# Attention stage of a hybrid block: both turns of a group behind y_b, and whole y_b products in every second group of some units

## The chip, the cores and the metric

The kernel runs on one core of one Trainium2 chip, in float32 (products are done on operands split in a high and a low part). The metric is the device time of the whole program in microseconds (us): the median of three runs, and beside it one execution taken by the hardware profiler. The engines are TensorE (PE; its weight loads are listed apart as PEld), VectorE (DVE), ScalarE (ACT), GpSimd (POOL) and SyncE (SP, which issues most of the DMAs).

## The reference, cut to what matters

One layer, a sequence of 2048 positions, model width 1024. Three groups of eight heads attend with a window and a dilation each; a recurrent branch runs beside them; both are projected, gated and merged.

```python
DILATION_GROUPS = ((128, 1), (512, 4), (2048, 16))
...
proj = x @ w_in[l] + b_in[l]
q, k, v, g_attn, u_lru, g_lru, gate_logits = jnp.split(proj, SPLIT_POINTS, axis=-1)
...
for g, (window, dilation) in enumerate(DILATION_GROUPS):
    o_g, lse_g = dilated_band_attention(q[:, :, g], k[:, :, g], v[:, :, g], window, dilation)
...
wts = jax.nn.softmax(jnp.stack(lses, axis=0), axis=0)
attn = jnp.sum(wts[..., None] * jnp.stack(outs, axis=0), axis=0)
attn = attn.reshape(B, S, ATTN_OUT_WIDTH).astype(dt) * jax.nn.silu(g_attn)
y_a = attn @ w_attn_proj[l]
...
y_b = (h * jax.nn.silu(g_lru)) @ w_lru_proj[l]
...
merged = gates[:, :, 0] * y_a + gates[:, :, 1] * y_b
out = merged @ w_out[l] + b_out[l]
x = layer_norm(DEEPNORM_ALPHA * x + out, ln_gain[l], ln_bias[l])
```

In `dilated_band_attention` a block of 128 queries meets the keys of its own block and of the one before it within its residue class, under a band mask; p = exp(s - m), l = sum p, o = p v. The outputs are divided and combined by weights from m and l.

## The kernel before

The program goes through the projection (L639 and its neighbours), then the attention stage (about 1453 to 1778 us of the span), then a stage that finishes y_b, then y_a, the output product and the layer norm. The change lies in the attention stage.

That stage works on 48 **groups** G of four query blocks for a pair of heads. Four groups are a **unit** u = G // 4: one head pair and one dilation group. Units with u % 3 = 0 and 2 have predecessor blocks (keys of two blocks, a band of 192 columns); units with u % 3 = 1, dilation 16, have none (128 columns), and neither have the first blocks of the others (one block of dilation 1, four of dilation 4). A group has two score jobs j = 2G, 2G + 1 of two blocks each. A job goes through these steps:

- `scores` (PE, L992 without and L998 with a predecessor) writes two banks of PSUM, tags "s0" and "s1", two buffers each.
- `weigh` (once for each block): DVE adds the mask and takes the maximum (L1012), ACT takes the exponential and the sum (L1014). The result lies in one of six p buffers PT in SBUF, cut from one tile PB.
- `turn_p` (PE, L1029) transposes p into two PSUM banks, tags "t0" and "t1" with one buffer each, or "s0" and "s1" at the last job. `copy_p` copies them to SBUF: e = 0 on ACT (L1042), e = 1 on DVE (L1044), or on ACT for the odd job of a group with spreads.
- `values` (PE, L1061) multiplies by V into the bank tagged "o" (one buffer), for two jobs at once, and DVE copies it out (L1077).

Once a unit, `turn_ml` transposes its maxima and sums (mlt, L1082), in the same "o" bank. From these, weights are made later, and `spread` (PE, L1155, into "s0" and "s1" banks) spreads them over the rows; DVE multiplies (L240) and POOL adds the three dilation groups up. At most two spreads lie in a group: in G = 19 to 25, 31 to 37 and 43 to 48.

Beside that the stage has pieces of **y_b**: 32 products n of 512 positions by 128 columns, each in two **halves** of twelve matmuls (`yb_part`, L1231; four parts of three). The bank tagged "y" takes one product. When it is complete DVE multiplies it by the gate (`yb_done`, L1241). `yb_care` loads what comes next: the weights of the next product, split by POOL (`split_wl`), and, during the last product of 512 positions (n = 7 and 15), the next eight h tiles, split by POOL (`split_h`, L1206 and L1207), behind which one group rests from y_b.

The order of the work is the order of the code in a loop over G; nothing is scheduled behind it. On each engine the instructions run in this order and wait for buffers and results of others. Before, a group runs on PE: turn of 2G - 2, scores of 2G and of 2G + 1, turn of 2G - 1, values of 2G - 3 and 2G - 2, one half of y_b (from G = 4 on, except in rests) with the spreads between its parts, mlt.

## Time and profile before

| what | value |
|---|---|
| median of 3 runs | 2117.38 us (2115.23 to 2119.68) |
| the profiled execution's own time | 2116.21 us |
| its span | 2114.3 us |
| scores' maxima, DVE L1012, whole stage | 216 of 353 ns and 168 of 287 ns |
| exponentials, ACT L1014, whole stage | 384, 421 ns |
| products with h, PE L1231, whole stage | 505, 402 ns |
| turns, PE L1029, whole stage | 1200, 229 ns |

The rows of the profile are read like this: a row of a timeline has its start, its length, the engine, the line, the operation, the output and the inputs by the program's names, the shapes, a count, and in brackets the idle time ahead of it and what ended it. "128*64" is the part of TensorE's array that a weight load takes. "issue" means that the profile shows nothing that the engine waited for. Times of a window are busy time within it.

### The profile page before, as it was taken

The page shows a single profiled execution, that of the slowest core. Times are in us where ns is not written, and L with a number is a line of the kernel's source. Part 1 is how long each engine was busy: PE and PEld are TensorE (multiplying, and loading weights), DVE is VectorE, ACT ScalarE, POOL GpSimd, SP SyncE. Part 2 cuts the span into 40 slices and gives each one's busy share as a digit, 9 for nine tenths or more (in the row PEclk, how much of TensorE's full clock was granted, in tenths as well). Part 3 has the DMA queues.
Part 4 walks back from the last instruction along what each step waited for, and adds up shares of the span by engine and source line. Part 5 has one row for each costly group of instructions (what it writes and reads, how often), then busy time and mean ns, then how long its engine had stood idle before and what let it go on. Part 6 is the DMA issues. An engine that isn't in the chain of part 4 may idle for free.

```text
span 2114.3 us, 35689 instructions
## 1 busy us (share of the span) xinstructions
PE 2093.4 (99%) x12069; PEld 1714.0 (81%) x12069; DVE 1650.2 (78%) x2937; ACT 1205.9 (57%) x2502; POOL 765.7 (36%) x685
## 2 busy tenths in 40 slices
PE   9999999999999999999999999999999999999998
PEld 7888888888888888888888888887788888788886
DVE  8787987988989768677777878875667767887667
ACT  6456556467457556677677787775666664321100
POOL 2544653653754301111111111112547678521120
PEclk9999999999999999999999999999999999999999
DMA  7876976876877866566655666669789886774431
GB/s 223 255 225 189 273 221 202 257 231 216 250 242 225 288 194 183 191 205 175 206 190 175 207 204 206 188 208 271 201 219 251 236 236 187 239 242 152 154 100 70
DMA packets 259077, 443.36 MB, mean 210 GB/s; under 512 B 64352, under 2 KB 92032, under 8 KB 255824
## 3 DMA queue, kind: packets, MB, share of 16 engines
q1 hardware_dynamic: 242256, 408.64, 61.7%
q0 software_dynamic: 11744, 23.54, 5.9%
q10 hardware_dynamic: 4896, 8.92, 1.1%
q8 instruction: 96, 1.57, 0.3%
q14 instruction: 85, 0.70, 0.1%
HBM read 290.00 MB, written 150.99 MB: 209 GB/s over the span
## 4 chain that ended last, share of the span: by engine, by line
PE 59%; DMA 4%; POOL 1%; DVE 1%; issue 1%; ACT 0%; SPq 0%; ACTq 0%; POOLq 0%; DVEq 0%
PE q L639 33%; PE yb L1231 6%; PE o L1061 3%; PE z L1536 3%; PE z L1538 3%; PE z L1537 3%; PE pt L1029 2%; PE s L998 2%; PE ya L1504 1%; PE ya L1505 1%; PE ya L1503 1%; DMA wor<-in_w_out_dram 1%; PE g L500 1%; PE s L992 1%; DMA war<-in_w_f_dram 1%; DMA hx<-hb_scr 1%
## 5 line engine op out<-in xcount | busy, mean ns | idle before, releaser
L639 PE MATMUL q<-xT,hS 128*128 128x512 f32 x1632 | 504.8, 390 | 0.0
L639 PE MATMUL q<-xT,l 128*128 128x512 f32 x1088 | 423.5, 389 | 0.0
L639 PE MATMUL q<-xB,hA 128*128 128x512 f32 x1344 | 417.8, 392 | 0.0
L639 PE MATMUL q<-xB,l 128*128 128x512 f32 x944 | 367.9, 390 | 0.0
L639 PEld LDWEIGHTS q<-xT,hS 128*128 128x128 f32 x1632 | 304.8, 188 | 64.4 <-issue 1.8
L639 PEld LDWEIGHTS q<-xB,hA 128*128 128x128 f32 x1344 | 250.6, 188 | 56.4 <-issue 5.5
L639 PEld LDWEIGHTS q<-xT,l 128*128 128x128 f32 x1088 | 204.2, 188 | 42.5
L240 POOL TENSOR_TENSOR sw<-sw,sin 128x512 f32<-128x512 f32 x96 | 156.4, 1635 | 167.6 <-ACT sw L329 94.7
L639 PEld LDWEIGHTS q<-xB,l 128*128 128x128 f32 x944 | 177.4, 188 | 37.3
L240 POOL TENSOR_TENSOR y<-y,h 128x512 f32<-128x512 f32 x28 | 39.2, 1401 | 384.1 <-DVE h L541 354.4
L1014 ACT ACTIVATE pb<-pb 128x192 f32<-128x192 f32 (+1 forms) x384 | 160.6, 421 | 26.1 <-DVE pb L1012 26.1
L639 PE MATMUL q<-xB,hS 128*128 128x512 f32 x544 | 168.7, 391 | 0.8 <-DVE v L240 0.8
L639 PE MATMUL q<-xT,hA 128*128 128x512 f32 x544 | 167.9, 390 | 0.0
L284 ACT ACTIVATE hA<-wA 128x512 fp32r<-128x512 f32 x220 | 138.5, 635 | 28.4 <-DVE l L240 11.4
L1231 PE MATMUL yb<-hx,wl 128*128 128x512 f32 x576 | 149.7, 400 | 1.0 <-POOL hx L1207 0.8
L284 ACT ACTIVATE hS<-S 128x512 fp32r<-128x512 f32 x170 | 108.3, 637 | 67.1 <-DVE S L240 47.5
L240 POOL TENSOR_TENSOR l<-wA,hA 128x512 fp32r<-128x512 f32 x68 | 110.2, 1621 | 84.5 <-ACT hA L284 49.5
L1231 PEld LDWEIGHTS yb<-hx,wl 128*128 128x128 f32 x576 | 104.5, 188 | 30.4 <-issue 5.6
L639 PEld LDWEIGHTS q<-xT,hA 128*128 128x128 f32 x544 | 101.8, 188 | 21.8 <-issue 0.8
L639 PEld LDWEIGHTS q<-xB,hS 128*128 128x128 f32 x544 | 101.2, 188 | 22.1 <-issue 1.6
L328 ACT ACTIVATE sw<-y 64x512 f32<-64x512 f32 x96 | 60.6, 631 | 83.5 <-DVE y L583 79.3
L1507 POOL TENSOR_TENSOR me<-gA,me 128x512 f32<-128x512 f32 x30 | 47.3, 1592 | 158.6 <-DVE gA L1506 135.9
(213 smaller groups left out, 4370.5 us busy)
## 6 DMA issues: line engine op xcount, KB each, us to landing
wA<-in_w_in_dram SPq DMA_DIRECT2D x220, 256.0 KB
wl_scr<-l SPq DMA_DIRECT2D x102, 512.0 KB
l<-wl_scr SPq DMA_DIRECT2D x102, 512.0 KB
wS<-in_w_in_dram SPq DMA_DIRECT2D x102, 256.0 KB
wS<-in_w_in_dram POOLq DMA_DIRECT2D x68, 256.0 KB, 7.0
wlr<-in_w_f_dram SPq DMA_DIRECT2D x64, 256.0 KB
mg_scr<-y SPq DMA_DIRECT2D x59, 256.0 KB
v_scr<-vs SPq DMA_DIRECT2D x48, 256.0 KB
```

The source lines that it names most:

```text
L240: eng.tensor_tensor(out=out, in0=in0, in1=in1, op=op)
L284: act.activation(heads(h), heads(r, False), AF.Copy)
L328: act.activation(flat(sw)[lo_], flat(rw)[up_], AF.Copy, scale=scale)
L639: pe.matmul(bank, w[:, ks], x[:, kk, xx], start=(first and i == 0), stop=(last and i == 11))
L998: pe.matmul(bank[h][es, b, 0:BW], q[hs, n * P + 64 * e:n * P + 64 * e + 64], k_[hs, at + 64 * e:at + 64 * e + BW], start=True, stop=True)
L1014: act.activation(pp, pp, AF.Exp, scale=-1.0, bias=mm, accum_out=ll)
L1061: pe.matmul(o[hs, 2 * i + b, :], V[:, kb, 64 * h:64 * h + 64], ptb[:, b, 2 * h + x, :], start=(x == lo // P), stop=(x == 1))
L1231: pe.matmul(YB["t"], w[:, a, k], hx(8 * c + k)[:, b], start=(hf == 0 and m == 0), stop=(hf == 1 and m == 11))
L1507: (dve if i in (6, 7) else pool).tensor_tensor(out=ME[c][:, f], in0=ga, in1=ME[c][:, f], op=ALU.add)
L1536: pe.matmul(z, mh[:, k], w[:, 0, hs], start=(k == 0), stop=False)
L1537: pe.matmul(z, mh[:, k], w[:, 1, hs], start=False, stop=False)
L1538: pe.matmul(z, ml[:, k], w[:, 0, hs], start=False, stop=(k == 7))
```

## The change

The loop's order on PE becomes: scores of 2G and of 2G + 1, values of 2G - 4 and 2G - 3, y_b with the spreads between its parts, mlt, then both turns, that of 2G - 2 in the "s" banks and that of 2G - 1 in the "t" banks. A job's values so come one to two groups later than before. There are eight p buffers in place of six; one of them lies in a new tile PX, which also takes the maxima and sums. Two buffers take the copied turns in place of three. In units with predecessors the odd groups have both halves of y_b and the even ones none; units without predecessors keep a half in each group. In all 44 halves lie in the stage in place of 42. The rests stay. All lines of the attention stage's functions stand three lower in the kernel after (L1012 becomes L1015).

```diff
@@ -915,7 +915,7 @@
     w_p = stC.enter_context(tc.tile_pool(name="w_p", bufs=1, reuse_waits="tile"))
     OT = [big(f"Z{i}", [P, 2, S], F32, f"o{i}") for i in range(3)]
     PB = big("Z3", [P, 4096], F32, "pb")
-    PT = [PB[:, 576 * i:576 * i + 576] for i in range(6)]
+    PT = [PB[:, 576 * i:576 * i + 576] for i in range(7)]
     BW = 192
 
     def pdata(p, h, a, b):
@@ -943,11 +943,14 @@
         x, y = ((2, 0), (2, 1), (1, 1))[i] if hp % 2 == 0 else ((0, 0), (0, 1), (1, 0))[i]
         return OT[x][:, y]
 
+    PX = at_p.tile([P, 576 + 256], F32, name="px", bufs=1)
+    PT.append(PX[:, 0:576])
+
     def zeros():
-        z = PB[:, 0:3456].rearrange("p (i c) -> p i c", c=576)
+        z = PB[:, 0:4032].rearrange("p (i c) -> p i c", c=576)
         for a in (0, 256, 512):
             dve.memset(z[:, :, a:a + 64], 0.0)
-        pool.memset(PB[:, 3456:3712], 0.0)
+        pool.memset(PX, 0.0)
 
     zeros()
 
@@ -1003,8 +1006,8 @@
         u, n = divmod(m, 16)
         bank, lo = st.pop(("s", m))
         if n == 0:
-            ML[u] = PB[:, 3456 + P * (u % 2):3456 + P * (u % 2) + P]
-        p = PT[m % 6]
+            ML[u] = PX[:, 576 + P * (u % 2):576 + P * (u % 2) + P]
+        p = PT[m % 8]
         cs, mk = (slice(lo, 256), mask) if lo else (slice(0, BW), band)
         for h in range(2):
             mm, ll = (ML[u][:, 32 * k + 16 * h + n:32 * k + 16 * h + n + 1] for k in range(2))
@@ -1017,7 +1020,7 @@
     def turn_p(j, tag="t"):
 
         pt = [aps.tile([P, 2, 4, 64], F32, tag=f"{tag}{e}", name=f"pt{e}{j}", bufs=1 if tag == "t" else 2) for e in range(2)]
-        ptb = at_p.tile([P, 2, 4, P], F32, tag="pt", name=f"ptb{j}", bufs=3)
+        ptb = at_p.tile([P, 2, 4, P], F32, tag="pt", name=f"ptb{j}", bufs=2)
         los = []
         for b in range(2):
             p, lo = st.pop(("p", 2 * j + b))
@@ -1333,59 +1336,61 @@
             spreads.setdefault(e + 7 + (i + (hp < 2)) // 2, []).append((hp, c, g))
 
     rests = set()
+    def turn(j, tag):
+        turn_p(j, tag)
+        copy_p(j, 0)
+        copy_p(j, 1)
+
     for G in range(NG + 1):
         run(late)
+        if G < GY or G in rests or G == NG:
+            m = 0
+        elif G // 4 % 3 == 1:
+            m = 1
+        else:
+            m = 2 * (G % 2)
+        now_ = [halves.pop(0) for _ in range(m)]
+        parts = [(*divmod(t, 2), i) for t in now_ for i in range(4)]
+
+        def some(k):
+            for _ in range(k):
+                if parts:
+                    n, hf, i = parts.pop(0)
+                    yb_part(n, hf, i)
+                    if i == 3 and hf:
+                        yb_done(n)
+
+        two = spreads.get(G, [])
         if G < NG:
-            if G:
-                turn_p(2 * G - 2)
-                copy_p(2 * G - 2, 0)
-                copy_p(2 * G - 2, 1)
             scores(2 * G)
             weigh(4 * G)
             weigh(4 * G + 1)
             scores(2 * G + 1)
-            if G:
-                turn_p(2 * G - 1)
-                copy_p(2 * G - 1, 0)
-                copy_p(2 * G - 1, 1)
             weigh(4 * G + 2)
             weigh(4 * G + 3)
-            if G:
-                values([j for j in (2 * G - 3, 2 * G - 2) if j >= 0])
-        else:
-            turn_p(2 * G - 2)
-            copy_p(2 * G - 2, 0)
-            copy_p(2 * G - 2, 1)
-            turn_p(2 * G - 1, "s")
-            copy_p(2 * G - 1, 0)
-            copy_p(2 * G - 1, 1)
-            values([2 * G - 3, 2 * G - 2])
-            values([2 * G - 1], "s0")
+        if G > 1:
+            values([2 * G - 4, 2 * G - 3])
         for fn in todo.pop(G, ()):
             fn()
-        y = G >= GY and G not in rests and (G < NG or len(halves) % 2)
-        if y:
-            n, hf = divmod(halves[0], 2)
-            yb_part(n, hf, 0)
-            yb_part(n, hf, 1)
-        two = spreads.pop(G, [])
+        some(1)
         if len(two) == 2:
             spread(*two[0], "s0")
-        if y:
-            yb_part(n, hf, 2)
+        some(2)
         if two:
             spread(*two[-1], "s1")
-        if y:
-            yb_part(n, hf, 3)
-            if hf:
-                yb_done(n)
+        some(9)
         if G % 4 == 0 and G:
             turn_ml(G // 4 - 1)
-        if y:
-            yb_care(halves.pop(0))
-            if hf and n in (7, 15):
+        if G:
+            turn(2 * G - 2, "s")
+            turn(2 * G - 1, "t")
+        spreads.pop(G, None)
+        for t in now_:
+            yb_care(t)
+            if t in (15, 31):
                 rests.add(G + 1)
         now["n"] += 1
+    values([2 * G - 2, 2 * G - 1])
     assert not todo and not spreads, (todo, spreads)
     now["n"] += 1
     run(late)
@@ -1447,7 +1452,7 @@
         rest.setdefault(16 + i, []).append(lambda: prep_wo(*wo.pop(0)))
     more = {(13, 15, 17, 19)[i]: [(3, c, g) for g in (0, 2, 1)] for i, c in enumerate(CO)}
     r0 = halves[0]
-    assert r0 == 42, r0
+    assert r0 == 44, r0
     for t in halves:
         n, hf = divmod(t, 2)
         run(late)
```

On ACT at G = 10 and 11 (ptb is the copy of a turn, with its job's number; pb and px are the p buffers) before:

```order
L1042 ACTIVATE ptb17_14884<-pt017_14882 128x4x64
L1014 ACTIVATE pb_13962<-pb_13962 128x192 x4
L1042 ACTIVATE ptb18_14936<-pt018_14934 128x8x64
L1014 ACTIVATE pb_13962<-pb_13962 128x192 x4
L1042 ACTIVATE ptb19_14985<-pt019_14983 128x8x64
L1014 ACTIVATE pb_13962<-pb_13962 128x192 x4
L1042 ACTIVATE ptb20_15056<-pt020_15054 128x8x64
L1014 ACTIVATE pb_13962<-pb_13962 128x192 x4
```

and now:

```order
L1045 ACTIVATE ptb16_14892<-pt016_14890 128x4x64
L1045 ACTIVATE ptb17_14905<-pt017_14903 128x4x64
L1017 ACTIVATE pb_13962,px_13975<-pb_13962,px_13975 128x192 x8
L1045 ACTIVATE ptb18_14982<-pt018_14980 128x8x64
L1045 ACTIVATE ptb19_15003<-pt019_15001 128x8x64
L1017 ACTIVATE pb_13962,px_13975<-pb_13962,px_13975 128x192 x6
L1017 ACTIVATE px_13975<-px_13975 128x192 x2
```

Before, a copy and four exponentials take turns; now the copies of both jobs stand behind the eight exponentials of the group.

On DVE at the end of a group with two spreads, G = 22 (ISA rows with a band are the maxima; w are the spread weights, gB the product with the gate) before:

```order
L1012 ISA pb_13962<-s045_16298,band_171 128x192
L1012 ISA pb_13962 128x1
L1012 ISA pb_13962<-s145_16299,band_171 128x192
L1012 ISA pb_13962 128x1
L1077 COPY o1_13960<-o41_16337 128x2x128 x2
L240 TENSOR_TENSOR o1_13960<-o1_13960,w011_16364 128x512
L240 TENSOR_TENSOR o2_13961<-o2_13961,w020_16370 128x512
L1241 SCALAR_TENSOR_TENSOR gB8_16056<-gB8_16056,yb10_16229 128x512
L1044 COPY ptb44_16387<-pt144_16386 128x8x64
```

and now:

```order
L1015 ISA pb_13962,px_13975<-s045_16284,band_171 128x192
L1015 ISA px_13975 128x1
L1015 ISA pb_13962,px_13975<-s145_16285,band_171 128x192
L1015 ISA px_13975 128x1
L1080 COPY o1_13960<-o40_16302 128x2x128 x2
L240 TENSOR_TENSOR o1_13960<-o1_13960,w011_16319 128x512
L240 TENSOR_TENSOR o2_13961<-o2_13961,w020_16322 128x512
L1047 COPY ptb42_16329<-pt142_16328 128x8x64
```

The products by w and the copy of a turn's e = 1 part follow the maxima as before. The copy belongs to the group's own last piece now (job 42 is turned at the end of G = 22; before, job 44's copy opens G = 23), and the gate's product, which closes a y_b product, has moved to the odd groups.

On PE at G = 12, the first of a unit, from the piece ahead of the values to the next turn (o are the values, yb the y_b product) before:

```order
L1029 MATMUL pt023_15214<-ident_161,pb_13962 128x64
L1029 MATMUL pt123_15215<-ident_161,pb_13962 128x64
L1029 MATMUL pt023_15214<-ident_161,pb_13962 128x64
L1029 MATMUL pt123_15215<-ident_161,pb_13962 128x64
L1061 MATMUL o21_15243<-ptb21_15105,V_13884 64x128 x8
L1061 MATMUL o21_15243<-ptb22_15169,V_13884 64x128 x8
L1231 MATMUL yb04_15264<-hx0_13964,wl_13963 128x512 x12
L1082 MATMUL mlt2_15277<-ident_161,pb_13962 128x128
```

and now:

```order
L1001 MATMUL s025_15172<-qk1_13921 64x192 x2
L1001 MATMUL s125_15173<-qk1_13921 64x192 x2
L1001 MATMUL s025_15172<-qk1_13921 64x192 x2
L1001 MATMUL s125_15173<-qk1_13921 64x192 x2
L1064 MATMUL o20_15190<-ptb20_15105,V_13884 64x128 x8
L1064 MATMUL o20_15190<-ptb21_15126,V_13884 64x128 x8
L1085 MATMUL mlt2_15211<-ident_161,px_13975 128x128
L1032 MATMUL pt022_15215<-ident_161,pb_13962 128x64
L1032 MATMUL pt122_15216<-ident_161,pb_13962 128x64
```

The values follow the scores and not a turn, and no y_b product stands between the values and mlt, which shares their bank.

## The prediction

> **What bounds the kernel now.** I read the page first: the span, the busy shares and the chain of work that ended last.
>
> ```profile
> span 2114.3 us, 35689 instructions
> PE 2093.4 (99%) x12069; PEld 1714.0 (81%) x12069; DVE 1650.2 (78%) x2937; ACT 1205.9 (57%) x2502; POOL 765.7 (36%) x685
> PEclk9999999999999999999999999999999999999999
> PE q L639 33%; PE yb L1231 6%; PE o L1061 3%; PE z L1536 3%; PE z L1538 3%; PE z L1537 3%; PE pt L1029 2%; PE s L998 2%; PE ya L1504 1%; PE ya L1505 1%; PE ya L1503 1%; DMA wor<-in_w_out_dram 1%; PE g L500 1%; PE s L992 1%; DMA war<-in_w_f_dram 1%; DMA hx<-hb_scr 1%
> ```
>
> TensorE is busy 99% of the span at full granted clock, and the chain runs almost wholly through its lines. So the time moves by what TensorE gets less or more to do, or by what it newly waits for. The change lies in the attention stage. The second view is the busy time by stretches of it:
>
> ```profile
> 1454.00:1500.00 46.00, 41.32 (x597) 33.00 (x591) 32.23 (x160) 34.04 (x147) 31.59 (x46) 1.00 0.90 263
> 1500.00:1550.00 50.00, 50.00 (x683) 40.04 (x680) 32.98 (x143) 32.34 (x130) 16.10 (x19) 1.00 0.76 193
> 1550.00:1600.00 50.00, 49.45 (x613) 40.37 (x617) 37.29 (x163) 35.29 (x151) 33.91 (x44) 1.00 0.88 246
> 1700.00:1750.00 50.00, 48.96 (x620) 40.19 (x613) 35.33 (x161) 34.50 (x148) 38.59 (x50) 1.00 0.81 232
> ```
>
> The columns are length, then PE, PEld, DVE, ACT and POOL busy. Behind the start TensorE has hardly an idle microsecond here (50.00 of 50), while DVE and ACT are busy for two thirds. There is slack on them on average; what counts is whether it lies where the new order needs it. The third view is the timeline of TensorE's weight loads in one group of a unit with predecessor blocks (G=10). A row's start against the next row's start is what a piece costs with the passage behind it.
>
> ```profile
> 1540.15 0.58 PEld L1029 LDWEIGHTS pt<-ident,pb 64*128 64x128 f32 x16 [0.35 <-issue]
> 1540.80 1.18 PEld L998 LDWEIGHTS s<-qk 64*64 64x64 f32 x32
> 1542.26 0.58 PEld L1029 LDWEIGHTS pt<-ident,pb 64*128 64x128 f32 x16 [0.28 <-issue]
> 1542.91 1.73 PEld L1061 LDWEIGHTS o<-ptb,V 128*64 128x64 f32 x32
> 1544.81 2.62 PEld L1231 LDWEIGHTS yb<-hx,wl 128*128 128x128 f32 x12 [0.17 <-issue]
> 1547.77 0.58 PEld L1029 LDWEIGHTS pt<-ident,pb 64*128 64x128 f32 x16 [0.35 <-issue]
> ```
>
> The group takes 1547.77 - 1540.15 = 7.62 us: turn 0.65, scores 1.46, turn 0.65, values 1.90, half a product 2.96. Between the first load of the scores (1540.80) and the next turn that needs their weights there are 6.97 us.
>
> **The change part by part.**
>
> *The turns side by side.* Before, each turn stands between two pieces of another kind. The one place of before with two turns in a row is the last group:
>
> ```profile
> 1773.05 1.07 PEld L1029 LDWEIGHTS pt<-ident,pb 64*128 64x128 f32 x32 [0.35 <-issue]
> 1774.19 2.60 PEld L1061 LDWEIGHTS o<-ptb,V 128*64 128x64 f32 x48
> ```
>
> Two take 1774.19 - 1773.05 = 1.14 us against 2 x 0.65: 0.15 less. The new passage from scores to values is not in the trace; scores to turn costs 0.28 of idle and values to y_b 0.17, so I set it equal to scores to turn (bounds: 0.1 either way per group). 28 groups in which full bands are turned: **-4.2** (bounds -1.5 to -7). In units without predecessors (half the transposes, and passages between scores and turn that are short already, 0.24 from turn to scores at 1579.97 below) nothing.
>
> *The whole product in one.* Two halves run together save one passage in and one out: 24 loads follow each other at (2.62 - 0.19)/11 = 0.22 us. One product alone has values to y_b, 0.17 idle, and y_b to turn, 0.35 idle; a pair of groups has these once less, and values to turn instead, say 0.2: about 0.32 a pair. Six pairs have an even group without spreads: **-1.9** (bounds 0 and -3.1).
>
> The Trainium skill, TensorEngine Tiling (Array Packing), Tiling Modes, states that changing the tiling mode drains TensorE. By that rule each passage between row shapes (64\*64, 64\*128, 128\*64, 128\*128 in the rows above) costs a drain and the change, which has fewer of them, gains; the rows agree in sign, 0.35 and 0.28 idle at changes of shape and none inside a piece. By the rule alone the kernel would be faster, which is the first rival below; the sum does not rest on it.
>
> *A stall that goes.* Late in the stage a second turn waits for ACT, which is held up by work on the denominators:
>
> ```profile
> 1721.31 0.58 PEld L1029 LDWEIGHTS pt<-ident,pb 64*128 64x128 f32 x16 [1.17 <-ACT ptb L1042]
> 1705.60 0.58 PEld L1029 LDWEIGHTS pt<-ident,pb 64*128 64x128 f32 x16 [0.41 <-ACT ptb L1042]
> ```
>
> In the new order both turns follow their own banks' last readers by a product's length: **-1.6** for the two (0 to -1.6).
>
> *What the groups without y_b now wait for.* This is the term that decides. ACT and DVE in the same group G=10:
>
> ```profile
> 1541.83 0.36 DVE L1012 CUSTOM_DVE_ANT_0 pb<-s,band 128x192 f32<-128x192 f32 x1
> 1544.54 0.35 DVE L1012 CUSTOM_DVE_ANT_0 pb<-s,band 128x192 f32<-128x192 f32 x1
> 1544.93 0.69 DVE L1077 COPY o<-o 128x512 f32<-128x512 f32 x1
> ...
> 1542.23 0.46 ACT L1014 ACTIVATE pb<-pb 128x192 f32<-128x192 f32 x1 [0.67 <-DVE pb L1012]
> 1544.00 0.58 ACT L1042 ACTIVATE ptb<-pt 128x512 f32<-128x512 f32 x1
> 1545.80 0.45 ACT L1014 ACTIVATE pb<-pb 128x192 f32<-128x192 f32 x1
> ```
>
> DVE's first maximum starts 1.03 us after the scores' first load (1540.80), eight take 8 x 0.28 = 2.25. ACT's first exponential starts 1.43 after it; eight take 8 x 0.44 = 3.5. In the new program ACT has all eight ahead of the copies out of the turned banks, and the first turn lies in the banks that the next group's second scores need. So those scores can't start before 1.43 + 3.5 + 0.58 (copy) + 0.15 (the signal, an estimate; mlt below starts 0.05 after the copy that it waits for has ended) = 5.65 us after this group's scores. A group with y_b is over 8 us long, so nothing waits. One without it has, to that point, scores 1.46 + values 1.90 + turns 1.14 + the first half of the next scores 0.59 = 5.09: it waits 0.56. Where the values are those of blocks without predecessors (1.02) it is 1.3. Groups 14, 26, 38: 0.6 each, 10: 1.3. Group 12 has the transpose of the maxima and denominators (mlt) ahead of the turns, in the bank of the values, so it waits for DVE's copy of them, 1.1 us in two pieces there: 1.2. Sum **+4.3**.
>
> Groups 8, 32 and 44 have the same mlt behind a unit without predecessors. How this looks the trace shows at G=20, the group that has no y_b already:
>
> ```profile
> 1579.97 0.32 PEld L1029 LDWEIGHTS pt<-ident,pb 64*128 64x128 f32 x8 [0.35 <-issue]
> 1580.21 0.98 PEld L992 LDWEIGHTS s<-qk 64*128 64x128 f32 x16
> 1581.11 0.38 PEld L1029 LDWEIGHTS pt<-ident,pb 64*128 64x128 f32 x8
> 1581.56 0.85 PEld L1061 LDWEIGHTS o<-ptb,V 128*64 128x64 f32 x16
> 1582.58 0.30 PEld L1155 LDWEIGHTS w<-wh,sel 128*128 128x128 f32 x2 [0.17 <-DVE pb L1012]
> 1583.87 0.14 PEld L1082 LDWEIGHTS mlt<-ident,pb 128*128 128x128 f32 x1 [0.99 <-DVE o L1077]
> 1582.78 1.04 DVE L1077 COPY o<-o 128x512 f32<-128x512 f32 x1
> ```
>
> mlt stands 3.66 us behind the scores, because DVE's copy of the values (1.04) comes behind eight maxima; TensorE idles 0.99 for it. With 0.90 of scores and 1.02 of values and nothing else ahead, the wait is 1.45 at 8; at 32 and 44 two spreads follow and their multiplications on DVE (0.69 each) hold the banks of the next scores: 1.8 each. Sum **+5.1**.
>
> Groups 22, 24, 34 and 46 have two spreads. The next scores need the spreads' banks back, that is DVE: 1.03 + 2.25 + copy 1.1 + 2 x 0.69 = 5.8 us. TensorE is there after 1.46 + 1.02 to 1.90 + 0.77 (spreads) + 1.14 = 4.4 to 5.3: waits of 1.45, 0.8, 1.45 and 1.45, **+5.2**. All twelve: **+14.5**. The bounds: nothing, if the copies come ahead of need, and about double, if each wait also delays the next group's exponentials beyond what its y_b hides.
>
> *Groups of units without predecessors.* These keep one half each, but their two turns now come last, and DVE has the closing product with the gate (0.69) and a copy (0.42) ahead of the next second scores where a product ends; eight such groups x 0.36 = **+2.8** (0 to 4).
>
> *The first product after the rest.* POOL splits the eight h tiles of the next 512 positions back to back:
>
> ```profile
> 1580.96 0.61 POOL L1206 CAST hx<-hx 128x512 fp32r<-128x512 f32 x1 [6.30 <-PE s L992]
> 1595.09 1.30 POOL L1207 TENSOR_TENSOR hx<-hx 128x512 fp32r<-128x512 f32 x1
> ...
> 1587.40 1.24 PEld L1231 LDWEIGHTS yb<-hx,wl 128*128 128x128 f32 x6 [0.17 <-POOL hx L1206]
> 1595.05 1.23 PEld L1231 LDWEIGHTS yb<-hx,wl 128*128 128x128 f32 x6 [0.17 <-POOL hx L1206]
> ...
> 1708.14 2.59 PEld L1231 LDWEIGHTS yb<-hx,wl 128*128 128x128 f32 x12 [0.17 <-POOL hx L1206]
> ```
>
> They end at 1596.4. Before, the product's second half starts at 1595.05 and needs the last tile at its end. As a whole product it starts at 1587 again and its last quarter would need it about 1592 + spreads: some 2.7 us of wait here (2.5 to 3.5); the same at the next such place, behind 1708.14, where POOL's joins stand between: 2 (0 to 5). **+4.7**.
>
> *Ends.* The last values follow the loop alone with their copy, 1.2 with mlt. At the start POOL sets 832 columns to zero in place of 256 ahead of the first maximum, which waits for it today:
>
> ```profile
> 1455.50 0.33 POOL L950 MEMSET pb<- 128x256 f32 x1
> 1455.87 0.29 DVE L1012 CUSTOM_DVE_ANT_0 pb<-s,mask 128x128 f32<-128x128 f32 x1 [0.72 <-POOL pb L950]
> ```
>
> From 0.33 for 256 columns some 0.5 to 0.7 more, and no turn fills the first groups: 1. Together **+2.2**. That two halves of y_b move from the next stage into this one is even: their work is the same, and the next stage's stalls are set by its own loads (0, ±1).
>
> **Sum**: gains 4.2 + 1.9 + 1.6 = 7.7; losses 14.5 + 2.8 + 4.7 + 2.2 = 24.2; net +16.5. The profiled execution took 2116.2 us (span 2114.3 and 1.9 around it); that gives 2132.7. It lies 1.2 under the median of the runs shown, 2117.4, so that a median would be 2133 to 2134. I predict 2133.
>
> **The rivals.** *Only the passages count* (faster). The waits rest on the sequence of ACT's and DVE's work against an interval of 5.1 us that I put together from pieces; were it 0.6 us longer, or did the turned banks come free earlier, the commonest wait would be gone, and at 1.5 us longer all. For: ACT is busy only 32 of 50 us. Against: the 0.99 us at G=20 is such a wait, seen. Then -7.7 plus 2 for the ends: about 2109 to 2112.
>
> *Half the waits* (about even). If the exponentials overlap better in the short group and POOL's tiles come in time, 7 + 2.5 + 2 remain against 7.7: +4, about 2120.
>
> *The waits grow* (slower still). If the delayed second scores also delay that group's exponentials, and the tiles of POOL come 5 us late at both places, 24 to 30 more: 2140 to 2146.
>
> *The change doesn't do what it says.* The two turns lie next to each other in the program and the products are whole in the odd groups; that leaves this out but for the start.
>
> **How the numbers follow.** A measurement of this kernel tells about 0.2%, 4.2 us, from no change. Forecast, waits about as summed (+9 to +24): 0.52. Half the waits (-3 to +9): 0.20. Only the passages (-10 to -3): 0.14. Growing waits (over +24): 0.14. Range 2111 to 2142, which leaves out most of the last and of the passages' case. Faster: 0.13; within 0.2%: 0.13, most of the half case; slower: 0.74.
>
> **What would show it.** Right: weight loads of the second scores (L998, L992) in odd groups idle 0.5 to 1.5 us for ACT's copy of the turned tile or DVE's product by w; mlt rows with 1 us or more behind DVE's copy of o; the product behind each rest waiting 2 to 3 us for POOL; pairs of turns at 1.14; PE's busy time in 50 us windows some 2 us under 50. Wrong: windows at 50.00 with scores that name no releaser, or a stall that names a DMA. My sum would be wrong first in the interval of a short group, since the same 0.5 us counts in twelve of them.

## The result, and the profile after

The kernel after takes 2134.24 us in the median of four runs (2132.99 to 2136.62), the kernel before 2117.49 beside it (2115.23 to 2119.68): a ratio of 1.0081, 95% interval 1.0068 to 1.0094. The change makes the kernel 17 us slower. Run again beside later experiments it gave 1.0085 (1.0071 to 1.0098). The span of the profiled execution went from 2114.3 to 2131.5, by 17.2.

From the page of after, the span, the busy shares and the chain of work that ended last:

```profile
span 2131.5 us, 35687 instructions
PE 2098.2 (98%) x12069; PEld 1715.4 (80%) x12069; DVE 1636.5 (77%) x2927; ACT 1204.3 (56%) x2500; POOL 770.6 (36%) x689
PE yb L1234 5%; PE z L1541 3%; PE z L1543 3%; PE z L1542 3%; PE o L1064 2%; PE pt L1032 1%; PE ya L1509 1%; PE ya L1510 1%; PE ya L1508 1%; POOL hx L1210 1%; PE s L1001 1%; PE s L995 1%; DMA ga<-ga_scr 0%; POOL hx L1209 0%; ACT pb L1017 0%
```

TensorE has as many matmuls and 5 us more of busy time, and its share falls by a point. The chain of before ran through TensorE and a few DMAs; POOL's split of h (L1209, L1210) and ACT's exponentials (L1017) are new in it. The windows (length, then PE, PEld, DVE, ACT and POOL busy, then the granted clock, the DMA share and GB/s) show where:

```profile
1500.00:1550.00 50.00, 46.26 (x666) 37.31 (x664) 32.94 (x150) 32.32 (x133) 11.69 (x14) 1.00 0.76 198
1550.00:1600.00 50.00, 47.93 (x521) 38.60 (x521) 29.70 (x134) 28.87 (x128) 35.53 (x47) 1.00 0.81 224
1700.00:1750.00 50.00, 47.73 (x640) 38.58 (x639) 29.51 (x125) 30.07 (x117) 41.43 (x53) 1.00 0.84 224
```

Where TensorE was busy for 50.00, 49.45 and 48.96 us of 50, it now is for 46.26, 47.93 and 47.73. The clock is granted in full in these windows (1.00), so these are waits.

The end of G=13, a group with a whole product, and G=14, one without, weight loads of TensorE in the timeline of after (G=14 begins at 1543.34, G=15 at 1547.63):

```profile
1536.66 5.31 PEld L1234 LDWEIGHTS yb<-hx,wl 128*128 128x128 f32 x24 [0.17 <-issue]
1542.33 0.95 PEld L1032 LDWEIGHTS pt<-ident,pb 64*128 64x128 f32 x28 [0.35 <-PE yb L1234]
1543.34 1.18 PEld L1001 LDWEIGHTS s<-qk 64*64 64x64 f32 x32
1544.80 1.51 PEld L1064 LDWEIGHTS o<-ptb,V 128*64 128x64 f32 x28 [0.28 <-issue]
1546.48 0.83 PEld L1032 LDWEIGHTS pt<-ident,pb 64*128 64x128 f32 x24 [0.17 <-issue]
1547.23 0.33 PEld L1032 LDWEIGHTS pt<-ident,px 64*128 64x128 f32 x8
1547.63 0.53 PEld L1001 LDWEIGHTS s<-qk 64*64 64x64 f32 x16
1548.81 0.53 PEld L1001 LDWEIGHTS s<-qk 64*64 64x64 f32 x16 [0.65 <-ACT ptb L1045]
```

The new order is seen: a whole product as 24 loads without a gap, then two turns in one, then scores. Behind the group without y_b the second scores idle 0.65 us for ACT's copy. ACT in the same stretch, its first and last exponential and the copies:

```profile
1544.66 0.45 ACT L1017 ACTIVATE pb<-pb,px 128x192 f32<-128x192 f32 x1 [0.55 <-DVE px L1015]
...
1547.75 0.44 ACT L1017 ACTIVATE pb<-pb,px 128x192 f32<-128x192 f32 x1
...
1548.19 1.05 ACT L1045 ACTIVATE ptb<-pt 128x512 f32<-128x512 f32 x2
```

Eight exponentials run without a gap from 1544.66 to 1548.19, the two copies follow at once, and the second scores start behind the first of them: 5.47 us behind the group's first load (1548.81 - 1543.34), against 5.65 in the prediction. The other kinds of wait in short groups, the product behind the rest, the last group, and a wait far behind the stage:

```profile
1502.56 0.14 PEld L1085 LDWEIGHTS mlt<-ident,px 128*128 128x128 f32 x1 [1.47 <-DVE o L1080]
...
1517.73 0.53 PEld L1001 LDWEIGHTS s<-qk 64*64 64x64 f32 x16 [1.30 <-ACT ptb L1045]
...
1531.90 0.14 PEld L1085 LDWEIGHTS mlt<-ident,px 128*128 128x128 f32 x1 [1.47 <-issue]
...
1596.63 0.30 PEld L1234 LDWEIGHTS yb<-hx,wl 128*128 128x128 f32 x2 [1.17 <-POOL hx L1210]
1597.18 0.19 PEld L1234 LDWEIGHTS yb<-hx,wl 128*128 128x128 f32 x1 [0.26 <-POOL hx L1209]
1598.53 0.30 PEld L1234 LDWEIGHTS yb<-hx,wl 128*128 128x128 f32 x2 [1.16 <-POOL hx L1210]
...
1604.69 0.20 PEld L1001 LDWEIGHTS s<-qk 64*64 64x64 f32 x4 [0.44 <-DVE o L240]
1605.28 1.17 PEld L1001 LDWEIGHTS s<-qk 64*64 64x64 f32 x28 [0.40 <-DVE o L240]
...
1791.89 1.75 PEld L1064 LDWEIGHTS o<-ptb,V 128*64 128x64 f32 x32 [0.57 <-ACT ptb L1045]
1795.10 0.14 PEld L1085 LDWEIGHTS mlt<-ident,px 128*128 128x128 f32 x1 [0.98 <-PE w L1158]
1797.01 1.76 PEld L1064 LDWEIGHTS o<-ptb,V 128*64 128x64 f32 x32 [0.57 <-ACT ptb L1045]
...
1885.81 0.19 PEld L1541 LDWEIGHTS z<-wo,ms 128*128 128x128 f32 x1 [1.04 <-ACT ms L1527]
```

At 1502.56 (G=8) mlt waits for DVE's copy of the values; the 1.47 at 1531.90 (G=12) is the same place, and there the profile names nothing. At 1604.69 (G=22) the scores' banks are held by DVE's products with the spread weights. At 1596.63 the whole product behind the rest waits for POOL's last two h tiles: 2.59 us. The last row is new beyond the stage: before has no wait of z for ACT's ms.

In two points the change is other than described. By the loops, the values of an even job come one group later than before, those of an odd job in the same group. And only the first rest stays at G=20; the second one, at G=37 before, falls on G=36 now.

### The profile page after: what moved, and what is told of

It is laid out like the page before. It is cut to its first block, busy times and chain, and to the rows that moved or that the text cites. A ratio compares the mean times of both kernels' runs of the same rounds, so it can differ in the third digit from the quotient of the medians.

```text
span 2131.5 us, 35687 instructions
## 1 busy us (share of the span) xinstructions
PE 2098.2 (98%) x12069; PEld 1715.4 (80%) x12069; DVE 1636.5 (77%) x2927; ACT 1204.3 (56%) x2500; POOL 770.6 (36%) x689
## 5 line engine op out<-in xcount | busy, mean ns | idle before, releaser
L284 ACT ACTIVATE hA<-wA 128x512 fp32r<-128x512 f32 x220 | 138.7, 636 | 28.7 <-DVE l L240 11.5
L1017 ACT ACTIVATE pb<-pb,px 128x128 f32<-128x128 f32 (+1 forms) x336 | 140.0, 418 | 16.0 <-DVE px L1015 15.2
L1234 PE MATMUL yb<-hx,wl 128*128 128x512 f32 x576 | 144.8, 398 | 3.7 <-POOL hx L1210 3.7
L240 DVE TENSOR_TENSOR S<-S,wA 128x512 f32<-128x512 f32 x102 | 96.5, 946 | 11.5 <-DMA wA<-in_w_in_dram 8.0
```

The lines of the kernel that those rows point to most:

```text
L240: eng.tensor_tensor(out=out, in0=in0, in1=in1, op=op)
L284: act.activation(heads(h), heads(r, False), AF.Copy)
L1017: act.activation(pp, pp, AF.Exp, scale=-1.0, bias=mm, accum_out=ll)
L1234: pe.matmul(YB["t"], w[:, a, k], hx(8 * c + k)[:, b], start=(hf == 0 and m == 0), stop=(hf == 1 and m == 11))
```

## The experiments

The theory: the loss comes from short groups, those without y_b, in which ACT and DVE can't finish what TensorE needs next, and from whole products that reach POOL's h tiles too early. The main rival was that the new place of the turns costs by itself. Each experiment was timed against runs of before on its own chip, so ratios are compared. Spans of profiled executions carry some us of their own: between executions with the same code, the start of the stage alone moved by 1 to 2, and the part behind the stage took 330.1 to 333.4 (after, after once more, and the third, fourth and fifth experiment). The kernel after was among the later ones once more, as a measure for them (1.0085, above):

> The kernel after, unchanged, beside the three that follow, so that they stand against it on one chip and against the same runs of before. Expected: the ratio to before at 1.007 to 1.009 again.

**The turns alone.**

```diff
-        if G < GY or G in rests or G == NG:
+        if G < GY or G in rests:
             m = 0
-        elif G // 4 % 3 == 1:
-            m = 1
+        elif G == NG:
+            m = len(halves) % 2
         else:
-            m = 2 * (G % 2)
+            m = 1
...
-    assert r0 == 44, r0
+    assert r0 == 42, r0
```

> The kernel after, but with one half of y_b in every group from 4 on, as before (rests as before, 42 halves in the stage); the turns stay together behind y_b, with the eight p buffers and PX. Theory (the loss comes from groups without y_b, in which ACT's eight exponentials and DVE's maxima and copies are not done in time): no such groups but the two rests, so the loss goes: passages -4, the 1.2 us stall at 1721 of before -1, against 0.9 at the start, about 1 in the groups without predecessors and 1 to 2 at the end: 2113 to 2119 us, no pair of scores waiting 0.5 us or more for the copy of a turn outside the rests. Rival (the new place of the turns costs by itself: values a job later, turned banks shared with the scores, two buffers for the copies): most of the 17 us stays, 2126 or more, with waits in groups with a half too.

2119.36 against 2115.52: 1.0020 (1.0011 to 1.0029), span 2116.2. By the ratios 13 of the 17 us are gone with the short groups, by the spans 15, so the rival falls. The theory was some 3 us too kind, and scores did wait for copies outside the rests: in the first groups (1.77 and 0.50) and once late in the stage, below. The passages do save what was said in full bands. The scores of groups 12 and 16 start in before and in this kernel at

```profile
1525.73 0.32 PEld L992 LDWEIGHTS s<-qk 64*128 64x128 f32 x4
...
1555.88 0.43 PEld L992 LDWEIGHTS s<-qk 64*128 64x128 f32 x6
```

```profile
1524.27 0.31 PEld L995 LDWEIGHTS s<-qk 64*128 64x128 f32 x4
...
1553.81 0.42 PEld L995 LDWEIGHTS s<-qk 64*128 64x128 f32 x6
```

that is 30.15 against 29.54 for four groups, 0.15 each. But the stall of before at 1721 did not go. It came back one piece later, and larger, since ACT's copies of both turns now stand behind the exponential of the weights (mt), which waits for POOL:

```profile
1718.68 0.52 PEld L995 LDWEIGHTS s<-qk 64*128 64x128 f32 x8 [1.56 <-ACT ptb L1045]
...
1717.63 0.52 ACT L1131 ACTIVATE mt<-mt 32x384 f32<-32x384 f32 x1 [3.39 <-POOL mt L240]
```

**Whole products alone.** The order of before, with the amounts of the change (and its places for the spreads, behind the first and the third part of y_b):

```diff
-        y = G >= GY and G not in rests and (G < NG or len(halves) % 2)
+        if G < GY or G in rests or G == NG:
+            m = 0
+        elif G // 4 % 3 == 1:
+            m = 1
+        else:
+            m = 2 * (G % 2)
...
-    assert r0 == 42, r0
+    assert r0 == 44, r0
```

> The kernel before in its order of turns, scores and values, with its six p buffers; only the amounts of y_b are those of the change (whole products in odd groups of units with predecessors, none in the even ones, 44 halves). Theory: a short group is there too, but the copies alternate with the exponentials, so that scores don't wait for a copy behind eight exponentials; what stays are the waits of mlt for DVE's copy of the values (five more groups, about 1 us each), those for POOL's h tiles (2.6 and 2.3) and something in groups with two spreads: 2123 to 2129, between the two. Rival A (the order of the turns makes the loss, whole products do not): 2113 to 2119. Rival B (whole products make all of it, whatever the order): 2132 or more.

2127.53, 1.0058 (1.0046 to 1.0070), span 2125.2: neither rival, but at the upper edge of what was expected. The rows show why the two parts together lose more (17.2) than each alone (10.9 and 1.9). The waits for ACT at the groups 10 and 11 are here

```profile
1514.96 0.58 PEld L1029 LDWEIGHTS pt<-ident,pb 64*128 64x128 f32 x16 [0.43 <-ACT ptb L1042]
1517.20 0.58 PEld L1029 LDWEIGHTS pt<-ident,pb 64*128 64x128 f32 x16 [0.41 <-ACT ptb L1042]
```

where after has 1.30 at one place, and groups 14, 26 and 38 have none: with copies between the exponentials a short group nearly suffices. In the groups 22 and 46 the scores wait 0.26 and 0.18 for DVE's product by w, where after has 0.84, and in 34 not at all. The waits of mlt and for POOL's h tiles are here much as in after.

**mlt at the start of its group.**

```diff
+        if G % 4 == 0 and G:
+            turn_ml(G // 4 - 1)
         if G < NG:
             scores(2 * G)
...
-        if G % 4 == 0 and G:
-            turn_ml(G // 4 - 1)
         if G:
             turn(2 * G - 2, "s")
```

> The kernel after, with mlt moved from behind y_b to the start of its group, ahead of the scores; it then finds its bank copied out long before. The rows of after show 1.47, 1.47, 0.91, 1.02, 0.91, 1.03, 0.90 and 0.98 us of idle ahead of mlt, 8.7 together. Theory (DVE and ACT are late in a short group as a whole, and mlt is only the first to meet them): the wait turns up at the next scores, behind ACT's copy or DVE's product by w; passages to and from mlt cost 0.3 each; net -1 to -3, 2131 to 2133.5. Rival (mlt's wait is a loss of its own): -6 to -8, 2126 to 2128.

2134.96, 1.0083 (1.0070 to 1.0095): no gain in the median. The waits of mlt are gone from the timeline, and at group 8 nearly all of it stands at the next group's second scores instead, behind ACT's copy:

```profile
1504.06 0.53 PEld L1001 LDWEIGHTS s<-qk 64*64 64x64 f32 x16 [1.30 <-ACT ptb L1045]
```

At 20, 32 and 44 the next scores wait 1.1 for DVE's product by w in place of 0.9 at mlt. So the rival (a loss of its own) falls for these: in a short group several engines are late together, and the one that is met first hides the next. Group 12 is the exception that the rows show. From the scores of G=11 to those of G=14 after takes 27.44 us and this kernel 26.38, and no wait comes back behind it.

The expected 1 to 3 us are not in the median. In the profiled execution, the slowest of the six (2139.47), the product behind the rest waited longer for POOL (0.61 + 1.16 + 1.16 + 0.97), and TensorE ran at half clock behind it, as the windows show:

```profile
1595.00:1600.00 5.00, 3.04 (x8) 1.48 (x7) 0.00 (x0) 0.00 (x0) 4.84 (x6) 0.80 1.01 195
1600.00:1605.00 5.00, 5.00 (x54) 3.25 (x56) 2.41 (x11) 2.01 (x8) 4.54 (x5) 0.52 1.04 349
```

Of the other five runs, two with a granted clock of 0.999 over the whole program took 2130.1 and 2130.9, and three with 0.996 to 0.998 took 2134.6 to 2137.4. That it was this place which lowered the clock in them is not shown.

**The product behind each rest in halves.**

```diff
-        elif G // 4 % 3 == 1:
+        elif G // 4 % 3 == 1 or G in (21, 22, 37, 38):
             m = 1
```

> The kernel after, with the first product behind each rest (n8, n16) as two halves in groups 21 and 22, 37 and 38, as before, in place of a whole one in 21 and 37. Theory: the waits for POOL's last h tiles (1.17 + 0.26 + 1.16 and 0.92 + 0.26 + 1.16 of idle in the rows of after) go, and those of groups 22 and 38 for DVE's product by w and for ACT's copy (0.8 and 0.65) go too, because these groups have a half; 0.3 is lost in each pair: -5 to -6.5, 2128 to 2129.5. Rival (POOL is late by the same time anyway and the next piece that needs it waits): -2 or less.

2125.9, 1.0048 (1.0036 to 1.0060): 7 us of after's 17, a little more than expected. From group 21 to 22 the loads run through:

```profile
1593.25 0.57 PEld L1032 LDWEIGHTS pt<-ident,pb 64*128 64x128 f32 x16 [0.35 <-PE yb L1234]
1593.89 1.18 PEld L1001 LDWEIGHTS s<-qk 64*64 64x64 f32 x32
1595.35 0.85 PEld L1064 LDWEIGHTS o<-ptb,V 128*64 128x64 f32 x16 [0.28 <-issue]
1596.37 0.53 PEld L1234 LDWEIGHTS yb<-hx,wl 128*128 128x128 f32 x3 [0.17 <-POOL hx L1209]
```

The half of y_b that moves to group 22 gives POOL the time, and nothing waits there or later for an h tile by more than the 0.17 of a plain passage. The rival falls.

**Two exponentials behind the copies.**

```diff
-            act.activation(pp, pp, AF.Exp, scale=-1.0, bias=mm, accum_out=ll)
+            if m // 4 in (10, 14, 26, 38) and m % 4 == 3:
+                behind.append((pp, mm, ll))
+            else:
+                act.activation(pp, pp, AF.Exp, scale=-1.0, bias=mm, accum_out=ll)
...
             turn(2 * G - 1, "t")
+        while behind:
+            pp, mm, ll = behind.pop(0)
+            act.activation(pp, pp, AF.Exp, scale=-1.0, bias=mm, accum_out=ll)
```

> The kernel after, but in the four short groups without spreads in which a pair of scores waited for ACT's copy (10, 14, 26, 38), the last block's two exponentials of eight stand behind the copies on ACT. Theory (the copy out of the turned bank is late because it stands behind all eight exponentials): the copy comes 2 x 0.44 = 0.88 us earlier, so the idle of 1.30 and 3 x 0.65 ahead of the second scores falls to about 0.4 and to the 0.2 or less of a plain passage; 2 to 2.6 us in all. Rival (these scores wait for DVE's copy of the other half of the turned tile, or for PE's own passages, and ACT is only the last one named): the same rows move by less than 0.2 each.

2127.94, 1.0058 (1.0044 to 1.0071), beside after's 1.0085. The rows at groups 10 and 14, where after has 1.30 and 0.65:

```profile
1514.68 0.78 PEld L1001 LDWEIGHTS s<-qk 64*64 64x64 f32 x16 [0.42 <-ACT ptb L1050]
...
1544.78 1.18 PEld L1001 LDWEIGHTS s<-qk 64*64 64x64 f32 x32
```

0.88 less at the one, nothing left at the other; 26 and 38 are as 14. Against after the scores come 0.67, 0.53, 0.54 and 0.55 us earlier over the four groups, 2.3 in all. That ACT's order makes these waits is shown. The rest of the 5.7 us that the ratios differ by is not in these rows. The spans differ by as much, and there 2.2 lie at the start of the stage and 1.8 behind it, which this edit doesn't touch, and 0.6 go to a longer wait for POOL at group 21.

**Repairs of the turns alone.** In the first experiment's kernel, the closing product with the gate and all steps of `todo` go behind the turns, PX is cleared in pieces, and the last group is reordered:

```diff
-                        yb_done(n)
+                        done.append(n)
...
-        for fn in todo.pop(G, ()):
-            fn()
...
             turn(2 * G - 1, "t")
+        if G == NG:
+            turn_ml(G // 4 - 1)
+        for n in done:
+            yb_done(n)
+        for fn in todo.pop(G, ()):
+            fn()
...
-    values([2 * G - 2, 2 * G - 1])
+    values([2 * G - 2, 2 * G - 1], "s0")
```

> The first experiment's kernel (turns together behind y_b, one half in each group) with its own waits taken away: the gate's product on DVE and the steps of the weights (ACT's exponential of them among them) stand behind the turns, so that the copies come first; at the last group mlt stands behind the turns and the last values use another bank; PX is set to zero in 256 columns by POOL and in three strips by DVE. Theory: what is left are the passages, 0.15 in each group with full bands, and the waits of the first experiment go (1.56 at group 40 for ACT, about 1 in units without predecessors, 1.5 of the 2.1 at the end): its span falls by 3 to 4.5 to 2112 to 2113.5, so 1 to 2 below before, ratio 0.998 to 1.0005. Rival (the turned banks are late for other reasons, or the steps of the weights come too late and the spreads wait): no better than the first experiment, 2116 or more.

2120.46, 1.0022 (1.0013 to 1.0031): no better than the first experiment, as the rival had it. The 1.56 at group 40 went (0.54 stand at 41), but the steps in `todo` also issue loads and POOL's work, and TensorE waits for POOL now:

```profile
1597.60 0.30 PEld L1235 LDWEIGHTS yb<-hx,wl 128*128 128x128 f32 x2 [1.05 <-POOL hx L1211]
1603.07 0.53 PEld L1235 LDWEIGHTS yb<-hx,wl 128*128 128x128 f32 x3 [0.49 <-POOL wl L1194]
```

That the moved steps make these waits is read from the rows; no run separates it.

**Repairs of the whole change**: the same, with the halves and the two exponentials of the experiments above (in 10, 14 and 26).

> The change with both parts kept and the waits found so far taken away together: halves in 21, 22, 37 and 38 (as in the fourth experiment), two exponentials behind the copies in 10, 14 and 26, and the repairs of the kernel above. Theory: the pieces add up, because they are waits at different places: -7 (fourth experiment) -2 (exponentials) -3 (repairs) from 2134: 2120 to 2124, ratio 1.002 to 1.004; what is left are mlt's and the spreads' waits in short groups, about 6. Rival (each wait removed shows up as another a group later): 2126 or more.

2146.91, 1.0143 (1.0130 to 1.0157): a plain miss, 13 us slower than after. A row of TensorE and three of POOL:

```profile
1565.12 4.77 PEld L1240 LDWEIGHTS yb<-hx,wl 128*128 128x128 f32 x12 [4.35 <-POOL wl L1199]
...
1560.33 1.40 POOL L240 TENSOR_TENSOR mt<-whl,mt 32x128 f32<-32x128 f32 x3 [32.50 <-DVE whl L240]
1562.37 2.15 POOL L240 TENSOR_TENSOR mt<-mt 32x384 f32<-32x384 f32 x3 [0.63 <-ACT mt L1137]
1564.47 0.60 POOL L1199 CAST wl<-wlr 128x512 fp32r<-128x512 f32 x1
```

POOL's steps of the weights, put back behind DVE's part of them, stand ahead of the split of the next product's weights (wl), and TensorE waits 4.35 us for that, at each of the three head pairs; behind it twelve loads take 4.77 us at a clock of 0.50 (3.75 and 3.76 at the other two places) where they take 2.6 elsewhere.

**Two repairs alone.** In the first experiment's kernel only the step with ACT's exponential stands behind the turns, beside the repair of the last group:

```diff
+            if i == 2:
+                behind[e + g] = lambda hp=hp, i=i: step(hp, i)
+            else:
+                at_group(e + g, lambda hp=hp, i=i: step(hp, i))
...
             turn(2 * G - 1, "t")
+        if G == NG:
+            turn_ml(G // 4 - 1)
+        if G in behind:
+            behind.pop(G)()
```

> The first experiment's kernel (turns together, one half in each group) with two of the repairs alone: only the step with ACT's exponential of the weights (groups 15, 27, 39) stands behind the turns, all other steps stay ahead of them; and the repair of the last group. The gate's product and PX are as in the first experiment. Theory (what undid the gains of the repaired kernel was that all steps, loads and POOL's work among them, came later, seen as 1.05 of wait for POOL's h tiles and 0.5 for its weights): -1.5 at group 40 and -1.2 at the end stay and nothing comes back: span 2113 to 2114, level with before within 0.1%. Rival (the repairs move the wait on to the next one, whatever they are): 2116 or more.

2115.07 against 2114.94: 0.9999 (0.9990 to 1.0008), span 2113.2. Level with before, as expected, but the rows don't show that the repairs made it so. The 1.56 at group 40 is gone. At group 43 a spread waits now, and at the end the first product of the next stage:

```profile
1740.15 0.19 PEld L1158 LDWEIGHTS w<-wh,sel 128*128 128x128 f32 x1 [1.01 <-DVE o L1080]
...
1779.03 5.97 PEld L1234 LDWEIGHTS yb<-hx,wl 128*128 128x128 f32 x27 [1.46 <-POOL h L1209]
```

From the scores of the last group to that product it is 15.55 us, and 15.44 in the first experiment: the repair of the last group moved its wait on, as the rival had it. From the scores of G=8 to that product this kernel takes 280.48 and the first experiment 281.11. The whole stage, from the first scores on, takes 326.97 here, 326.18 there and 324.76 in before. Of the 3.0 by which the span is shorter than in the first experiment, 2.7 lie behind the stage (334.17 against 336.86), where the code is the same. So the stage is still longer than in before, and why the timed runs are level stays open. No kernel of this study is faster than before by more than can be measured.

**The change with these two repairs**: both parts, halves in 21, 22, 37 and 38, two exponentials behind the copies in 10, 14 and 26, and the two repairs above.

> Both parts of the change with the repairs that held: halves in 21, 22, 37, 38, two exponentials behind the copies in 10, 14, 26, and the two repairs of the kernel above; the steps of the weights stay ahead of the turns but for ACT's exponential. Theory (the repaired change lost 4.35 us three times because POOL's steps of the weights stood ahead of the split of the next product's weights, and half speed behind it; the rest of its pieces add up): 2122 to 2126, ratio 1.003 to 1.005, no wait of y_b for POOL's split of weights. Rival (in whole products any repair of the turns makes the split late): the 4.35 us come back, 2135 or more.

2127.77, 1.0063 (1.0049 to 1.0077): between theory and rival, and above what was expected. The 4.35 us did not come back in full, but a quarter of them did, at three places:

```profile
1561.18 2.61 PEld L1239 LDWEIGHTS yb<-hx,wl 128*128 128x128 f32 x12 [1.21 <-POOL wl L1198]
```

And at the end the 1.46 for POOL stands here too. So the pieces don't simply add up: by this row, POOL's queue has no room for a step of ACT that comes later when products are whole.

## Why the prediction was right

It said 2133 us, and 2134 were measured, and most of the loss is the mechanism that it named: short groups, and POOL's h tiles. That the sum is so near is partly luck. By its own terms:

- *The turns side by side* (-4.2): two full turns and the passage to the next scores take 1547.63 - 1546.48 = 1.15 us in after, against 1.14 predicted. In the first experiment four groups with full bands gain 0.61. But the starts of the groups show this gain only in units with dilation 1. In those with dilation 4, where one group in four has no predecessors, next to nothing is left once the later values and turns are allowed for. About -2.5 (an estimate from these starts), inside the bounds; the term was too large. The rule of the Trainium skill weighed there (TensorEngine Tiling (Array Packing), Tiling Modes: a change of mode drains TensorE) agrees in sign; the time did not come out by it.
- *Whole products* (-1.9): between groups 26 and 28, with the waits taken away in the fifth experiment, the pair takes 1643.70 - 1629.39 = 14.31 us; before it took 15.08 (1622.76 to 1637.84). Of the 0.77, turns explain 0.30 and the product, with 0.32 predicted, most of the rest.
- *A stall that goes* (-1.6): gone in after, where both turns stand behind a whole product, but not through the order of the turns: with that alone it was 1.56. The term was also too large, because 0.28 of each of its two idles is the plain passage from scores to a turn. Against groups of the same kind, G=40 takes 1.0 more in before and G=38 takes 0.1 more, 1.1 together.
- *Short groups* (+14.5): the idle rows of the twelve are 1.47 (8), 1.30 (10), 1.47 (12), 0.65 (14), 0.84 (22), 1.02 (24), 0.65 (26), 0.91 (32), 0.81 (34), 0.65 (38), 0.90 (44) and 0.84 (46): 11.5. The three kinds are there, and the price was about right where ACT's queue or mlt alone set it. It was too high with two spreads: 1.45 against 0.84 and 0.81 (22, 34, 46), and 1.8 against 0.91 and 0.90 (32, 44), where mlt waits and the scores behind it hardly do. Group 24 waits at mlt and not, as predicted, at the scores. Two of the prices don't follow from their own pieces: group 10, with values of 1.02, comes to 5.65 - 4.21 = 1.44 and not 1.3, and group 24 to 5.8 - 5.3 = 0.5 and not 0.8. Group 36, where the second rest falls now, waits 1.03 at mlt, for which no term stands. That four of these waits are made by ACT's order is shown by the fifth experiment. That DVE's products by w wait longer in the new order is shown by the second; what on DVE makes it is only read from the rows.
- *Units without predecessors* (+2.8): the first scores of groups 18 to 20 lie 5.57 and 5.79 apart in before, 5.84 and 5.90 in after: 0.27 and 0.11 a group in place of 0.36 in every second one, some 2 us in all (an estimate). No row of these groups names DVE, so that the wait which the term has in mind makes this is not shown.
- *POOL's h tiles* (+4.7): 1.17 + 0.26 + 1.16 at the one place, 0.92 + 0.26 + 1.16 at the other, 4.9 together, and the fourth experiment took them away.
- *Ends* (+2.2): the last group waits 0.57 + 0.98 + 0.57 = 2.1 alone, against 1.2; the start costs about 0.9 (an estimate), and part of that is a lower clock, which the term doesn't have (last section).
- *The next stage*, put at 0 ± 1: from its first product to the end of the span it is 336.42 in before and 332.57 in after, with two halves of y_b, 5.5, fewer: some 1.6 longer in this pair of profiles. As executions with the same code differ by up to 3.3 there, the term is not shown to be wrong. New is the wait of z for ms, 1.04 in after. All seven other profiles with 44 halves in the stage have it too, 0.6 in the third experiment and 1.2 to 1.6 in the others; none of the four with 42 has it.

The gains were priced too high and the waits too, and the sum came out right partly because these errors cancelled. With the whole products as predicted, these pieces give -2.5 - 1.9 - 1.1 + 11.5 + 1.0 + 2 + 4.9 + 3 + 1.6 = 18.5, against 16.5 predicted and 17.2 between the spans; the 1.3 too much lie within what the estimates among them leave open.

## What to carry to other kernels

A kernel whose bound engine is busy 99% of the time may leave others idle for a third of the time (here DVE was busy for 33 and ACT for 32 of 50 us) and still have no room: what counts is the interval between one piece and the next that needs its result. Before work is bunched, work out the shortest such interval that this leaves, and lay the other engines' queues beside it in their order (here 5.1 us against eight exponentials and a copy). And a step that is moved takes all its queues along: two repairs moved steps that only ACT was meant to leave, and TensorE then waited for POOL's splits. A repair is also to be judged by where the wait goes: that of the last group took 2.1 us of idle away and met 1.46 at the next piece.

## What was not expected of the hardware

TensorE's granted clock fell to half without a long pause. In the third experiment it was busy for 3.04 of 5 us between 1595 and 1600, in pieces between waits of at most 1.16, and behind that the clock was 0.52 for the next 5 us. In the second it was busy for 3.01 of 5 at the same product (1593 to 1598), and the clock was 0.50 from 1598 to 1600. After has two such waits, of 1.17 and 1.16, at this place, is busy for 3.40 of 5, and keeps its clock (1.00, third from the right). The fifth experiment has three, of 0.55, 1.16 and 1.16, is busy for 3.16 of 5, and keeps it too:

```profile
1594.00:1599.00 5.00, 3.40 (x14) 2.00 (x12) 0.34 (x1) 0.00 (x0) 4.84 (x6) 1.00 1.00 225
...
1591.00:1596.00 5.00, 3.16 (x11) 1.57 (x10) 0.00 (x0) 0.00 (x0) 4.84 (x6) 1.00 1.00 227
```

These four executions so lie close to a limit, but they don't show where it is.

After itself loses its clock at another place, the start of the stage. The scores of G=1 stand there behind an idle of 2.75 us; before idles 2.25 ahead of its first turn. The windows of before and of after:

```profile
1456.00:1460.00 4.00, 2.69 (x44) 1.80 (x44) 3.48 (x23) 3.80 (x18) 0.00 (x0) 1.00 1.03 333
...
1456.00:1460.00 4.00, 3.11 (x36) 2.25 (x38) 3.71 (x27) 3.71 (x17) 0.00 (x0) 0.70 1.03 324
```

Every other profile with both turns behind y_b has such a fall between 1455 and 1465; before and the second experiment, with the old order, have none.

The Trainium skill, TensorE: Matmul & The Clock Gate, What's actually happening, puts the fall to half speed behind an idle window of about 3.4 us; no single idle here was that long, so a stretch that is idle in good part suffices, which is nearer to what the same page says under A second HAM failure mode. Waits in short succession can so cost more than their rows show. In the third experiment waits of 3.9 us in all are followed by some 7 us at half clock, in which TensorE is busy for 6.8: at most 3.4 us on top (an estimate, half of the busy time).
